# A hybrid attention and delta-rule layer on one core: one chain of delta steps becomes one for each pair of heads, with banks of its own, and input products are computed before their job's phase and places are there

## The chip, the core and the metric

The kernel runs on one NeuronCore of a Trainium2 chip. TensorE multiplies, VectorE and ScalarE do elementwise work and read the accumulator (PSUM, 8 banks of 128 partitions x 512 fp32), GpSimd does elementwise work between tiles in SBUF, and the sync engine (SP) issues nearly all DMAs. The metric is the device time of one execution in microseconds, lower is better. TensorE's clock is throttled at times; the profile gives the granted share.

## What is computed

One layer of a streaming encoder, in fp32, for 2048 prompt frames and 32 sample frames (which have a cache and a state). Both kinds of frames go through one input projection of 6160 columns. Branch A is attention over a band of 576 keys, branch B a gated delta rule in chunks of 64 frames:

```python
qa, ka, va, za, qkv_b, zb, a_b, b_b, gate_a, gate_b = split_projection(x @ w_in)
ya = (band_attention(qa, ka, va) * silu(za)) @ w_branch_a
c = silu(causal_conv(qkv_b)); q, k = l2_normalize(c[q]), l2_normalize(c[k])
m = (k * beta) @ k.T * decay * strict                 # per chunk and head
t_inv = inverse(eye + m); u = t_inv @ (v * beta); w = t_inv @ (k * beta * exp(gc))
def step(s, chunk):                                    # in order over the chunks of a head
    v_new = u - w @ s
    o = (q * exp(gc)) @ s + (q @ k.T * decay) @ v_new
    s = s * exp(g_last) + (k * exp(g_last - gc)).T @ v_new
yb = (rms_norm(o) * silu(zb)) @ w_branch_b
y = layer_norm(ALPHA * x + (sigmoid(gate_a) * ya + sigmoid(gate_b) * yb) @ w_out)
```

## The kernel before

**Halves and phases.** The frames come in two halves of 1024; the 32 sample frames ride with the second. For each half the program opens phase B (`phase_b`, delta rule), runs it to its end, then opens phase A (`phase_a`, attention). After that come the branch projections, the merge and the output projection (`merge`).

**The order is written by a planner when the program is built.** Each activity is a Python generator, a stream with a clock of its own. `Flow.run` always continues the stream whose clock is lowest; an instruction that it issues is appended to its engine's program and moves the stream's clock on by a price. So the planner's clocks set the order of each engine's instructions, and on the chip each engine goes through that order. A stream that yields a `Gate` takes a place (a buffer, a PSUM bank) or waits until one is given back; a `Mark` is an event that it waits for.

**Input products.** `all_jobs` lists jobs of 128 output columns in a fixed order: for each half two or three gate jobs, the job `ab` (decay and beta), the conv jobs of branch B (q, k, v, z for each of the four pairs of heads p) with gate jobs between, six gate jobs, the sixteen jobs of branch A, the rest of the gate jobs. `fetch` loads a job's weights, `divide` splits them into two fp16 parts (`whi`, `wlo`), and `multiply` computes it in blocks of frames: a block is 24 matmuls into a bank `pj` (hi x whi, hi x wlo, lo x whi). There are two such banks. A block's evacuation is a stream of its own that gives the bank back. Counted over the program, the first half's phase B owns blocks 1 to 62, its phase A and the last gate jobs blocks 63 to 100, and the second half's phase B blocks 101 to 195.

A job that belongs to a phase has a key. Before its first block `multiply` itself waits until that phase is open and until the job's places are free (two places `raw_slots` for conv jobs; places for the keys, values, queries and z of branch A).

**Branch B.** `conv` makes q, k, v of a pair (p) and of 512 frames: one of two `Block`s k per pair and half, in all eight per half and one for the sample. `prep` makes decays, `system` the 64x64 systems (block-diagonal tiles `k_bd`, `qk_bd`), `side` the tiles `q_bd`, `kd_bd` and the values `v_t`. `solve` (two streams) inverts the 32x32 halves by substitution on VectorE (`sys_t`, `sys_u`; the data goes over DRAM buffers `sol_p` and `sol_u` to get one row per system), and `inverse` puts the inverse together (`u_bd`) with small matmuls in two banks, one of kind `a` and one of kind `b`. `chain`, one stream for all blocks in `order` (pair after pair), does the steps; `tail` scales and normalises the outputs (square on ScalarE, sums on VectorE, powers and the scaling on GpSimd), transposes them (`ident`, `v_t`) on TensorE, multiplies by z and stores. The last tail ends the phase. Buffers of branch B are chosen by the block's number (`k.n % NSIDE`, `k.n % NPAR`), so they come free in that order.

A step of the chain is, with the name of the tile that each result goes to:

```python
PE.matmul(xs[:, 0:HD], k.kb[:, c, :], st, start=True, stop=True)      # a <- state, k_bd
PE.matmul(os_[:, 0:HD], k.qb[:, c, :], st, start=True, stop=False)    # a <- state, q_bd
V.scalar_tensor_tensor(out=r[:], in0=xs[:, 0:HD], ...)                # r
PE.matmul(ys[:, 0:HD], k.ub[:, c, :], r[:], start=True, stop=True)    # a <- r, u_bd
V.tensor_scalar(out=vn[:], in0=ys[:, 0:HD], ...)                      # vn
PE.matmul(ds_[:, 0:HD], k.kdb[:, c, :], vn[:], start=True, stop=True) # c <- vn, kd_bd
PE.matmul(os_[:, 0:HD], k.qkb[:, c, :], vn[:], start=False, stop=True)# a <- vn, qk_bd
V.scalar_tensor_tensor(out=st, in0=st, ..., in1=ds_[:, 0:HD], ...)    # state
S.copy(out=vc, in_=os_[:, 0:HD])                                      # v_t <- a
```

There are 64 steps in the first half and 68 in the second (four are the sample's). "A hop" below is the way from one of these matmuls over VectorE to the next: over r, over vn, over the state.

**Banks.** The eight banks are set for the whole program: two `pj`, three `a`, two `b`, one `c`. In phase B the chain, the inverse and the tails use `a`, and the systems, the transposes, the weights' scales and the inverse use `b`.

Nearly every instruction is recorded through a helper, so the profile gives line 243 for all of them; the tiles' names tell them apart.

Of the kernel before, what the change touches and what calls it, by code (L numbers as in the profile page):

```python
# [81 lines left out]
class Gate:  # L82
# [169 lines left out]
def trunk(ctx: ExitStack, tc: tile.TileContext, x_p, x_s, cache_k, cache_v, st_conv, st_gdn,  # L252
# [24 lines left out]

    def mark():
        return Mark(flow)
# [5 lines left out]
    banks = {"pj": 2, "a": 3, "b": 2, "c": 1}  # L285
    bank = {k: gate(n) for k, n in banks.items()}

    def pt(tag):

        return psum.tile([P, 512], F32, tag=tag, bufs=banks[tag], name=tag)  # L290
# [252 lines left out]
    class Job:  # L543
# [3 lines left out]
        def __init__(self, half, wid, src, evac=None, key=None, cols=P, blocks=None):  # L547
            self.wid = wid
            self.half, self.src, self.evac, self.cols, self.key, self.slots = half, src, evac, cols, key, ()
# [67 lines left out]

    def multiply():

        while True:  # L620
            some, todo = [], [(0, 0)]
            while todo:
                bi, which = todo.pop(0)
                if which == len(some):
# [36 lines left out]
                flow.start(job.evac(bi, c0, n, gcol, ps))  # L661
# [78 lines left out]
    def phase_b(half):  # L740

        stack = ExitStack()
        bp = stack.enter_context(tc.tile_pool(name=f"bp{half}", bufs=1, reuse_waits="tile"))
# [28 lines left out]
        pd = [dram.tile([32, 1024], F32, name=f"sol_p{half}{i}") for i in range(NSIDE)]  # L772
        ud = [dram.tile([32, 1024], F32, name=f"sol_u{half}{i}") for i in range(NSIDE)]
# [8 lines left out]
        def block(p, b):  # L782
# [4 lines left out]
            k.prep, k.side = mark(), mark()  # L787
# [27 lines left out]
        par_slots, side_slots, u_slots = gate(NPAR), gate(NSIDE), gate(NSIDE)  # L815
        e_slot, tail_slot, p_slots, vt_slots = gate(1), gate(2), gate(NSIDE), gate(NSIDE)
# [177 lines left out]
        def prep():  # L994
            yield decay_done
            for k in order:
# [24 lines left out]
                k.sc = bp.tile([P, 4, 8], F32, tag="sc", bufs=7, name="sc")  # L1021
# [46 lines left out]
        def side(k, ss):  # L1068
# [5 lines left out]
            yield side_slots  # L1074
            k.qb, k.kdb = q_bd[k.n % NSIDE], kd_bd[k.n % NSIDE]
# [27 lines left out]
            yield vt_slots  # L1103
            k.v_t = bp.tile([P, 8, HD], F32, tag="v_t", bufs=NSIDE, name="v_t")
# [17 lines left out]
        def system(k):  # L1122
# [3 lines left out]
            yield par_slots  # L1126
            yield k.qk_ready
            yield k.prep
            yield p_slots
            kb, qkb = k.kb, k.qkb = k_bd[k.n % NPAR], qk_bd[k.n % NPAR]  # L1130
# [1117 lines left out]
```

## Time and profile before

| | us |
|---|---|
| median of 3 runs | 2180.49 |
| lowest, highest | 2174.0, 2183.27 |
| the profiled execution, its own time | 2178.3 |
| its span | 2176.2 |

By the trace, phase B of the first half goes to about 556 us, phase A of the first half to about 862, phase B of the second half to about 1412, and phase A of the second half to about 1800, where the merge has already begun. The rows of the profile are read like this: a group's row has the engine, the operation, tile out <- tiles in, shapes and count, then the busy time, the mean duration of one in ns, and the idle time of the engine just before them with what ended it. A row of the waits is the waiting engine and tile <- what it waited for: the sum, the number of waits, the longest. A row of the windows is a stretch, its length, the busy time and number of instructions for PE, PEld (weight loads), DVE (VectorE), ACT (ScalarE) and POOL (GpSimd), the granted clock of TensorE, the DMA engines' share and GB/s. A row of the timeline is a start, a duration and an instruction, with the wait before it in brackets. An fp32 matmul is recorded as two passes (x2).

### The profile page before, as it was taken

How to read it: one execution, taken by the hardware profiler on the slowest of the kernel's cores; microseconds unless marked ns; L12 is line 12 of the kernel's file. 1: busy time of each engine (PE TensorE's matmuls, PEld its weight loads, DVE VectorE, ACT ScalarE, POOL GpSimd, SP SyncE). 2: the span in 40 equal slices, each digit the busy share in tenths (PEclk: the TensorE clock that was granted, in tenths of full speed). 3: DMA queues.
4: the chain of work that ended last, by engine and by line, in shares of the span. 5: the costliest groups of instructions: out<-in, count | busy, mean ns of one | idle time of the engine just before them, and what ended most of it. 6: DMA issues, size and time to landing. Idle time of an engine off the chain costs nothing. (4 is left out here: it accounts for less than half of the span.)

```text
span 2176.2 us, 41392 instructions
## 1 busy us (share of the span) xinstructions
PE 2008.7 (92%) x15098; PEld 1436.2 (66%) x15098; DVE 1539.9 (71%) x4660; ACT 983.9 (45%) x2098; POOL 634.5 (29%) x708
## 2 busy tenths in 40 slices
PE   4898999999899999898999998899899998999998
PEld 4454665666465556565767776666676777988896
DVE  7689878874377657769887877437557577776676
ACT  5654545444366667554443533345556552111110
POOL 6343333322312123332233331310110214443333
PEclk9999999999999999999999999999999999999999
DMA  3223332332323223122223233231321526443331
GB/s 119 71 83 104 77 86 61 88 88 83 91 77 109 78 88 99 65 69 61 81 58 95 65 91 84 84 107 45 92 68 53 153 76 205 142 129 108 117 104 59
DMA packets 197719, 196.49 MB, mean 90 GB/s; under 512 B 79622, under 2 KB 147570, under 8 KB 197516
## 3 DMA queue, kind: packets, MB, share of 16 engines
q1 hardware_dynamic: 197516, 193.85, 30.4%
q8 instruction: 119, 1.95, 0.4%
q14 instruction: 84, 0.69, 0.1%
HBM read 135.91 MB, written 50.53 MB: 86 GB/s over the span
## 5 line engine op out<-in xcount | busy, mean ns | idle before, releaser
L243 PE MATMUL pj<-hi,whi 128*128 128x512 f16 (+2 forms) x1992 | 659.5, 346 | 16.4 <-ACT raw L243 7.8
L243 PE MATMUL pj<-hi,wlo 128*128 128x512 f16 (+2 forms) x1952 | 649.1, 345 | 0.4 <-POOL wlo L243 0.4
L243 PEld LDWEIGHTS <-whi 128*128 128x128 f16 x3984 | 412.4, 105 | 226.0 <-issue 17.7
L243 PE MATMUL pj<-lo,whi 128*128 128x512 f16 (+2 forms) x1992 | 450.2, 341 | 0.0
L243 POOL TENSOR_TENSOR wlo<-wraw,whi 128x512 f16<-128x512 f32 x192 | 227.9, 1188 | 696.7 <-ACT whi L243 421.5
L243 PEld LDWEIGHTS <-wlo 128*128 128x128 f16 x1952 | 204.7, 105 | 119.9 <-issue 20.9
L243 ACT CAST mh<-sg 128x256 fp32r<-128x256 f32 x64 | 25.9, 406 | 276.0 <-DVE sg L243 276.0
L243 DVE TENSOR_TENSOR sys_u<-sys_u,sys_t 128x60 f32<-128x60 f32 (+24 forms) x527 | 134.2, 255 | 18.5 <-DVE sys_t L243 0.2
L243 ACT ACTIVATE wraw<-wraw,w_scale 128x1024 f32<-128x1024 f32 (+1 forms) x98 | 111.5, 1137 | 63.1 <-DVE w_scale L243 62.6
L243 PE MATMUL a<-ghi,whi 128*128 128x256 f32 (+1 forms) x512 | 132.3, 289 | 7.6 <-DVE sg L243 7.4
L243 ACT CAST whi<-wraw 128x512 f16<-128x512 f32 (+1 forms) x196 | 119.3, 611 | 30.6 <-PE pj L243 28.0
L243 ACT CAST ph<-b 128x512 f16<-128x512 f32 (+2 forms) x224 | 92.9, 422 | 86.8 <-PE b L243 78.9
L243 PE MATMUL a<-ghi,wlo 128*128 128x256 f32 (+1 forms) x512 | 130.2, 285 | 0.6 <-DVE wlo L243 0.5
L243 DVE TENSOR_TENSOR pl<-b,ph 128x512 f16<-128x512 f32 (+2 forms) x224 | 106.8, 484 | 26.3 <-ACT ph L243 25.6
L243 DVE TENSOR_TENSOR sys_t<-sys_u,sys_p 128x60 f32<-128x60 f32 (+21 forms) x459 | 118.4, 258 | 4.7
L243 ACT ACTIVATE sb<-sb,mx,unit 128x640 f32<-128x640 f32 (+4 forms) x128 | 108.8, 851 | 27.7 <-DVE mx L243 25.8
L243 DVE SCALAR_TENSOR_TENSOR acc<-raw,cwT,acc 128x512 f32<-128x512 f32 x144 | 113.2, 786 | 6.0 <-ACT acc L243 5.0
L243 ACT COPY v_t<-a 128x64 f32<-128x64 f32 x132 | 27.9, 211 | 192.6 <-PE a L243 184.0
L243 POOL TENSOR_TENSOR w_scale<-w_scale,mhalf 128x1 f32<-128x1 f32 x49 | 30.3, 618 | 287.3 <-DVE w_scale L243 219.2
L243 PE MATMUL b<-ident,sb 128*128 128x128 f32 x560 | 100.0, 279 | 14.1 <-ACT sb L243 6.2
L243 PEld LDWEIGHTS a<-ghi,whi 128*128 128x128 f32 x512 | 97.7, 191 | 9.6 <-DVE sg L243 8.5
L243 PEld LDWEIGHTS a<-ghi,wlo 128*128 128x128 f32 x512 | 97.3, 190 | 1.3 <-DVE wlo L243 1.0
(356 smaller groups left out, 4270.5 us busy)
## 6 DMA issues: line engine op xcount, KB each, us to landing
wraw<-in_w_in SPq DMA_DIRECT2D x192, 256.0 KB
sg<-sig SPq DMA_DIRECT2D x112, 128.0 KB
sig<-sig SPq DMA_DIRECT2D x44, 256.0 KB
sys_p<-sol_p SPq DMA_DIRECT2D x17, 512.0 KB
x<-in_x_p SPq DMA_DIRECT2D x16, 512.0 KB
xt<-in_x_p SPq DMA_DIRECT2D x16, 512.0 KB
out_y_p<-xt SPq DMA_DIRECT2D x16, 512.0 KB
glo<-g SPq DMA_DIRECT2D x14, 512.0 KB
```

What stands on the lines that cost most here:

```text
L243: r = f(*a, **k)
```

## The change

**Banks by phase.** Only `pj` and `b` (two each) stay for the whole program. The other four are opened with a stage: three `a` at the start and three `a` and one `c` in phase A as before, and in phase B two `x` and two `o`.

**A chain for each pair of heads.** The single stream becomes four (one for each pair's two blocks) and one for the sample. A chain takes one of two numbered places before a block and with it one bank `x`, in which the step's three results have columns of their own, and one bank `o` for the output. The two matmuls on the output, and ScalarE's copy, are no longer issued by the chain but by short streams beside it (`outputs`). Since blocks can now end in another order, buffers are handed out as numbered places and given back by number, the buffers in DRAM are one for each block, and three small tiles have more buffers.

**Products before phase and places.** `multiply` no longer waits for a job's phase and places. It starts a stream that does (`open_job`), and the block's evacuation waits for that, with its bank.

**The inverse** uses one bank `b` for both heads in place of an `a` and a `b`, and the tails use `b`.

```diff
+class Places(Gate):
+    def __init__(self, flow, n):
+        super().__init__(flow, n)
+        self.numbers = deque(range(n))
+    def take(self):
+        yield self
+        return self.numbers.popleft()
+    def back(self, i):
+        self.numbers.append(i)
+        self.give()
...
-    banks = {"pj": 2, "a": 3, "b": 2, "c": 1}
+    banks = {"pj": 2, "b": 2}
...
+    def open_job(job):
+        go, make = phases[job.key[0]][job.half]
+        yield go
+        job.evac, slots = make[0](*job.key[1:])
+        for g in slots:
+            yield g
+        job.open.done()
+
+    def evac(job, *block):
+        if job.key:
+            yield job.open
+        yield from job.evac(*block)
...
                     if job.key:
-                        go, make = phases[job.key[0]][job.half]
-                        yield go
-                        job.evac, job.slots = make[0](*job.key[1:])
-                    for g in job.slots:
-                        yield g
+                        job.open = mark()
+                        flow.start(open_job(job))
...
-                flow.start(job.evac(bi, c0, n, gcol, ps))
+                flow.start(evac(job, bi, c0, n, gcol, ps))
...
+        open_banks(stack, f"psb{half}", x=2, o=2)
...
-        pd = [dram.tile([32, 1024], F32, name=f"sol_p{half}{i}") for i in range(NSIDE)]
+        pd = [dram.tile([32, 1024], F32, name=f"sol_p{half}{i}") for i in range(2 * NP)]
...
-            yield side_slots
-            k.qb, k.kdb = q_bd[k.n % NSIDE], kd_bd[k.n % NSIDE]
+            k.sn = yield from side_slots.take()
+            k.qb, k.kdb = q_bd[k.sn], kd_bd[k.sn]
...
-            banks_ = []
+            yield bank["b"]
+            ps = pt("b")
             for h in range(2):
                 r0 = h * HD
-                yield bank["ba"[h]]
-                ps = pt("ba"[h])
-                banks_.append(ps)
...
+        def outputs(m, x, os_, vc=None, end=None):
+            PE.matmul(os_, m, x, start=vc is None, stop=vc is not None)
+            yield
+            if vc is not None:
+                S.copy(out=vc, in_=os_)
+                if end:
+                    end.done()
+
-        def chain():
-            for k in order:
+        def chain(some):
+            for k in some:
                 yield k.ready
+                xn = yield from x_banks.take()
...
+                xs, ys, ds_ = (xb[xn][:, i * HD:(i + 1) * HD] for i in range(3))
+                os_ = ob_[xn][:, 0:HD]
                 for c in range(k.nch):
...
+                    PE.matmul(xs, k.kb[:, c, :], st, start=True, stop=True)
+                    yield
+                    r = bp.tile([P, HD], F32, tag=f"r{xn}", bufs=2, name="r")
+                    V.scalar_tensor_tensor(out=r[:], in0=xs, scalar=k.negc[:, c:c + 1], in1=vc, op0=ALU.mult, op1=ALU.add)
+                    yield
+                    PE.matmul(ys, k.ub[:, c, :], r[:], start=True, stop=True)
+                    flow.start(outputs(k.qb[:, c, :], st, os_))
+                    yield
+                    vn = bp.tile([P, HD], F32, tag=f"vn{xn}", bufs=2, name="vn")
+                    V.tensor_scalar(out=vn[:], in0=ys, scalar1=sc[:, 1, c:c + 1], scalar2=None, op0=ALU.mult)
+                    yield
+                    PE.matmul(ds_, k.kdb[:, c, :], vn[:], start=True, stop=True)
+                    flow.start(outputs(k.qkb[:, c, :], vn[:], os_, vc, k.out if c == k.nch - 1 else None))
+                    V.scalar_tensor_tensor(out=st, in0=st, scalar=sc[:, 3, c:c + 1], in1=ds_, op0=ALU.mult, op1=ALU.add)
+                    yield
+                yield k.out
+                x_banks.back(xn)
...
-        for g in (worker(todo), worker(decays), prep(), local(), solve(), solve(), chain()):
+        for g in (worker(todo), worker(decays), prep(), local(), solve(), solve()):
             flow.start(g)
+        for some in blocks + ([[sample]] if last else []):
+            flow.start(chain(some))
```

What this does to the order of TensorE is seen at two places. The first is the end of the first half's phase B. Before, these are the last matmuls of the chain (its last step and a part of the one before) and the last tail's transposes, with the first product of branch A behind them:

```order
L243 MATMUL b<-w_sq,tiny 128x1
L243 MATMUL c<-vn,kd_bd_618 128x64
L243 MATMUL a<-vn,qk_bd_608 128x64
L243 MATMUL a<-state,k_bd_600 128x64
L243 MATMUL a<-state,q_bd_612 128x64
L243 MATMUL a<-r,u_bd_624 128x64
L243 MATMUL c<-vn,kd_bd_618 128x64
L243 MATMUL a<-vn,qk_bd_608 128x64
L243 MATMUL a<-ident,v_t 128x128 x4
L243 LDWEIGHTS whi
L243 MATMUL pj<-hi_147,whi 128x512
```

Now the last step of the chain stands among products:

```order
L259 MATMUL o<-state,q_bd_619 128x64
L259 LDWEIGHTS whi
L259 MATMUL pj<-hi_150,whi 128x512
L259 MATMUL x<-vn,kd_bd_625 128x64
L259 LDWEIGHTS wlo
L259 MATMUL pj<-hi_150,wlo 128x512
L259 MATMUL o<-vn,qk_bd_615 128x64
L259 LDWEIGHTS whi
L259 MATMUL pj<-hi_150,whi 128x512
```

and the transposes of the last tail follow 35 products later:

```order
L259 LDWEIGHTS whi
L259 MATMUL pj<-lo_153,whi 128x512
L259 MATMUL b<-ident,v_t_655 128x128 x4
L259 LDWEIGHTS whi
L259 MATMUL pj<-lo_153,whi 128x512
```

What moved: the steps' two last matmuls, on `kd_bd` and `qk_bd`, are apart, and products stand between the chain's end and the transposes. At that place 62 blocks of products had been begun before and 60 are now; at the last transposes of the second half 195 before and 191 now.

The second place is a change from one block to the next in the middle of the first half, with the buffers' numbers. Before, the last step of a block (`c_4421`, `a_4396`) ends before the next block's first matmul (`a_4435`):

```order
L243 MATMUL c_4421<-vn_4415,kd_bd0_616 128x64
L243 MATMUL a_4396<-vn_4415,qk_bd3_608 128x64
L243 LDWEIGHTS whi_4017
L243 MATMUL pj_4403<-hi01_149,whi_4017 128x512
L243 LDWEIGHTS wlo_4018
L243 MATMUL pj_4403<-hi01_149,wlo_4018 128x512
L243 LDWEIGHTS whi_4017
L243 MATMUL pj_4403<-hi01_149,whi_4017 128x512
L243 LDWEIGHTS wlo_4018
L243 MATMUL pj_4403<-hi01_149,wlo_4018 128x512
L243 MATMUL a_4435<-state_118,k_bd0_594 128x64
```

Now the next block's first step (in bank `x_659`) stands beside the last step of the block before (in bank `x_660`):

```order
L259 MATMUL x_660<-state_118,k_bd3_607 128x64
L259 LDWEIGHTS whi_3829
L259 MATMUL pj_4084<-lo00_151,whi_3829 128x512
L259 MATMUL x_659<-state_118,k_bd0_601 128x64
L259 LDWEIGHTS whi_3829
L259 MATMUL pj_4084<-lo00_151,whi_3829 128x512
L259 MATMUL x_660<-r_4189,u_bd0_629 128x64
L259 LDWEIGHTS whi_3829
L259 MATMUL pj_4084<-lo00_151,whi_3829 128x512
L259 MATMUL o_662<-state_118,q_bd0_617 128x64
L259 MATMUL x_659<-r_4197,u_bd1_631 128x64
```

What moved: two blocks have a step beside each other here. Over the whole of the first half the first matmuls of the steps come as eight of one block, then eight of the next, as before.

More of the change, by code (lines that the diff above doesn't have):

```diff
@@ L1102, in side @@
             yield from by_token(k.qk[:, 1, :], nch, put_k)
-            yield vt_slots
-            k.v_t = bp.tile([P, 8, HD], F32, tag="v_t", bufs=NSIDE, name="v_t")
+            k.vn = yield from vt_slots.take()
+            k.v_t = v_ts[k.vn]
             yield bank["b"]
@@ L1205, in inverse @@
         def inverse(k, t):
-            yield u_slots
-            k.ub = u_bd[k.n % NSIDE]
+            k.un = yield from u_slots.take()
+            k.ub = u_bd[k.un]
             nch, ub, p_c = k.nch, k.ub, k.p_c
-            u0 = ud[k.n % NSIDE][:]
+            u0 = ud[k.n % (2 * NP)][:]
             yield t
@@ L1361, in tail @@
                 yield t
-            vt_slots.give()
+            vt_slots.back(k.vn)
             if k.p is None:
@@ L1367, in tail @@
             tail_slot.give()
-            if k is order[-1]:
+            left[0] -= 1
+            if not left[0]:
                 done.done()
```

101 lines of the change are left out of this document (45 added, 56 removed).

## The prediction

> **What bounds the kernel now.** I read the page first, then the table of windows cut at the borders of the stages, then the waits and the timeline at the places that these point to.
>
> ```profile
> span 2176.2 us, 41392 instructions
> PE 2008.7 (92%) x15098; PEld 1436.2 (66%) x15098; DVE 1539.9 (71%) x4660; ACT 983.9 (45%) x2098; POOL 634.5 (29%) x708
> ```
>
> TensorE is busy for 2008.7 of 2176.2 us. So all that this change can win is in the other 167.5 us, in time at a lower clock, and in matmuls that take longer than they must. It acts in the two stages of branch B, from about 100 to 562 us and from about 900 to 1414 us:
>
> ```profile
> 200.00:440.00 240.00, 220.64 (x1591) 145.65 (x1590) 203.48 (x715) 115.26 (x236) 76.22 (x103) 0.96 0.32 82
> 440.00:545.00 105.00, 101.22 (x784) 69.38 (x783) 60.89 (x250) 42.74 (x92) 30.26 (x31) 0.98 0.29 85
> 545.00:562.00 17.00, 9.34 (x38) 5.32 (x39) 5.39 (x19) 4.42 (x9) 9.33 (x9) 0.70 0.34 96
> ...
> 1010.00:1150.00 140.00, 129.53 (x1056) 95.78 (x1054) 125.63 (x428) 65.29 (x144) 42.72 (x63) 0.93 0.27 74
> 1150.00:1350.00 200.00, 187.64 (x1586) 143.67 (x1585) 156.56 (x565) 81.09 (x186) 58.70 (x75) 0.96 0.31 82
> ...
> 1400.00:1414.00 14.00, 7.87 (x45) 4.52 (x44) 6.60 (x21) 3.08 (x6) 7.71 (x8) 0.76 0.25 69
> ```
>
> The columns after the length are the busy time of PE, PEld, DVE, ACT and POOL, then the granted clock. Each stage has three parts. In the first, VectorE is nearly as full as TensorE: 203.48 of 240 us beside 220.64, and 125.63 of 140 beside 129.53. In the second, VectorE has room (60.89 of 105 us in the first half's stage) and TensorE alone sets the pace. In the third, 545 to 562 and 1400 to 1414, neither is full: the input products are used up and TensorE waits for the last block's tail. So a term that takes work from TensorE pays fully in the second part only, and work of VectorE that moves from the second part into the first costs up to its whole length.
>
> **The change, term 1: the waits at the end of both stages go.**
>
> ```profile
> 544.70:555.60 10.90, 3.09 (x19) 2.38 (x18) 4.69 (x18) 4.72 (x9) 5.53 (x5) 0.76 0.27 84
> 555.60:561.40 5.80, 5.73 (x18) 2.67 (x19) 0.88 (x2) 0.00 (x0) 3.80 (x5) 0.57 0.41 94
> 561.40:565.00 3.60, 3.60 (x18) 1.65 (x17) 0.00 (x0) 0.69 (x1) 0.00 (x0) 1.00 0.13 51
> ...
> 1402.20:1408.30 6.10, 0.04 (x1) 0.00 (x0) 2.66 (x8) 2.46 (x5) 3.88 (x4) 0.90 0.27 66
> 1408.30:1413.10 4.80, 4.73 (x24) 2.61 (x25) 2.85 (x10) 0.00 (x0) 3.82 (x5) 0.50 0.32 109
> ```
>
> ```profile
> 555.67 1.11 PE L243 MATMUL a<-ident,v_t 128*128 128x128 f32 x4 [6.60 <-POOL v_t L243]
> 1408.37 1.60 PE L243 MATMUL a<-ident,v_t 64*64 64x64 f32 x16 [6.13 <-POOL v_t L243]
> ```
>
> Both rows are transposes of a tail, which wait for the tail's scaling on GpSimd. In the old order of TensorE nothing stands between the last delta step of the first half and these transposes, and all 62 blocks of products of that stage are already behind it; in the second half it is 195 of 195. The next product belongs to branch A, and it waited for the phase. In the new order 35 product matmuls stand between the last step and the last transposes of the first half, and 36 and 45 before those of the sample rows. A product takes 0.2 us at the full clock (3.60 us for 18), so 35 are 7.0 us, against the 6.60 us of the wait; the last two steps, which stood bare, have products between them too. In the second half most products are narrower, so 36 and 45 of them may leave 1 or 2 us of the 6.13. What is gained: idle 10.90 − 3.09 = 7.8 us and 6.10 − 0.04 = 6.1 us, and the work after them at a lower clock, 5.73 × (1 − 0.57) = 2.5 us and 4.73 × (1 − 0.50) = 2.4 us. Together **−18.7 us**. What is late next there is nothing: branch A's first scores wait for products 70 and 207 in both orders, which TensorE now reaches sooner by as much.
>
> On the lower clock the rows have 5.8 and 4.8 us at about half speed behind each wait. The Trainium skill, "TensorE: Matmul & The Clock Gate", section "Part 1: The HAM clock gate", says that the full clock returns after one busy window of about 3.4 us. By that an estimate of each wait's aftermath would be 1.7 us and the term −17.3 us; the trace's longer stretch decides here.
>
> **Term 2: two matmuls of a step no longer stand side by side.**
>
> ```profile
> 302.85 0.36 PE L243 MATMUL c<-vn,kd_bd 128*128 128x64 f32 x2
> 303.05 0.39 PE L243 MATMUL a<-vn,qk_bd 128*128 128x64 f32 x2
> 303.27 0.38 PE L243 MATMUL pj<-hi,wlo 128*128 128x512 f16 x1
> ...
> 304.14 0.33 PE L243 MATMUL a<-state,k_bd 128*128 128x64 f32 x2
> 304.31 0.38 PE L243 MATMUL pj<-hi,wlo 128*128 128x512 f16 x1
> ```
>
> ```profile
> L243 PE MATMUL c<-vn,kd_bd 128*128 128x64 f32 x264 | 52.7, 282 | 16.1 <-DVE vn L243 11.3 <-DVE w_scale L243 4.4
> L243 PE MATMUL a<-vn,qk_bd 128*128 128x64 f32 x264 | 52.5, 282 | 0.0
> L243 PE MATMUL a<-r,u_bd 128*128 128x64 f32 x264 | 48.9, 268 | 23.0 <-DVE r L243 17.8 <-DVE sys_t L243 3.7 <-ACT zb L243 0.8
> L243 PE MATMUL a<-state,k_bd 128*128 128x64 f32 x256 | 44.7, 257 | 1.5 <-DVE state L243 1.2
> L243 PE MATMUL a<-state,q_bd 128*128 128x64 f32 x256 | 44.4, 256 | 0.1
> ```
>
> A step's matmul on kd_bd and the one on qk_bd followed each other and hold TensorE from 302.85 to 303.27, 0.42 us. One of the same shape between two products holds it for 0.17 us (304.14 to 304.31), so two apart take 0.34. The new order has them apart in all 132 steps, nearly always with a product between. That is 132 × 0.08 = 10.6 us by these rows; by the groups it is (52.7 + 52.5) − (44.7 + 44.4) × 264/256 = 13.3 us. I take 13 as the whole, and count half, **−6.5 us**, because in the first part of each stage TensorE's own time isn't what ends last. The other half is the bound below.
>
> **Term 3: VectorE's work comes earlier.** I counted the chain's steps and the finished systems in both orders at the same block of products. At block 54 of the first half there were 42 steps and now are 49, and one system more is finished (each system is one run of sys_t and sys_u); at block 188 it is 129 steps for 120, and half a system more.
>
> ```profile
> L243 DVE TENSOR_SCALAR vn<-a,sc 128x64 f32<-128x64 f32 x132 | 37.0, 280 | 31.3 <-PE a L243 29.8
> L243 DVE SCALAR_TENSOR_TENSOR r<-a,negc,v_t 128x64 f32<-128x64 f32 x132 | 37.0, 280 | 31.4 <-PE a L243 29.6
> L243 DVE TENSOR_TENSOR sys_u<-sys_u,sys_t 128x60 f32<-128x60 f32 (+24 forms) x527 | 134.2, 255 | 18.5 <-DVE sys_t L243 0.2
> L243 DVE TENSOR_TENSOR sys_t<-sys_u,sys_p 128x60 f32<-128x60 f32 (+21 forms) x459 | 118.4, 258 | 4.7
> ```
>
> A step has three operations like the first two rows (the third updates the state), 3 × 0.28 = 0.84 us; a system takes (134.2 + 118.4) / 17 = 14.9 us. So 7 × 0.84 + 14.9 = 20.8 us of VectorE's work come forward in the first half and 9 × 0.84 + 7.5 = 15.0 us in the second, 35.8 us in all, out of the part where they lay beside products into the part where VectorE is nearly full. What hides them there is VectorE's idle time, 36.5 us (240 − 203.48) and 43.4 us (200 − 156.56). That this is real room is seen in what it waits for:
>
> ```profile
> DVE state L243 <- PE c L243: 19.5, 32, 1.9
> DVE r L243 <- PE a L243: 18.4, 23, 1.6
> DVE vn L243 <- PE a L243: 13.1, 19, 1.6
> DVE sys_t L243 <- DMA sys_p<-sol_p: 10.0, 3, 4.1
> ```
>
> These are VectorE's waits from 100 to 556 us. 51.0 us of them are for TensorE, in 74 short pieces, and a VectorE that is later finds TensorE's result there. The bounds are 0 and +35.8 us. Since the room is twice the work, I take a quarter, **+9 us**.
>
> **Term 4: hops of the chain with less beside them.**
>
> ```profile
> 544.22 0.33 PE L243 MATMUL a<-state,k_bd 128*128 128x64 f32 x2
> 544.59 0.28 DVE L243 SCALAR_TENSOR_TENSOR r<-a,negc,v_t 128x64 f32<-128x64 f32 x1 [0.97 <-PE a L243]
> 545.02 0.41 PE L243 MATMUL a<-r,u_bd 128*128 128x64 f32 x2 [0.24 <-DVE r L243]
> ```
>
> Here, with VectorE free, the hop from one matmul of a step over VectorE to the next takes 0.80 us, and 0.24 of it is a wait. In the old order 44 of the 395 hops have under 0.5 us of TensorE's work between their matmuls, in the new one 66 have. With two products there (0.17 + 2 × 0.2 = 0.57 us) up to 0.23 us is missing: 22 × 0.23 = 5 us. A hop can also turn out better, where VectorE's queue puts the operation sooner. Bounds −4 and +8; I take **+3 us**.
>
> **What I cost at nothing.**
>
> ```profile
> PE pj L243 <- ACT raw L243: 4.4, 1, 4.4
> L243 ACT ACTIVATE wraw<-wraw,w_scale 128x1024 f32<-128x1024 f32 (+1 forms) x98 | 111.5, 1137 | 63.1 <-DVE w_scale L243 62.6
> ```
>
> An evacuation that waits for its place now holds one of the two product banks, and the product after next is queued behind it on TensorE. But that wait is there before as well (first row, 960 to 1415 us: a product waits 4.4 us for the evacuation into raw), because the same tile has to be free; only what stands beside it in the order differs. A chain now keeps one accumulator: its matmul on q_bd waits for ScalarE's copy of the step before, and behind it stand one product and the chain's next matmul. The copy has the rest of a step, some 2 us, and ScalarE is 45% busy; behind its longest operation (1.14 us, second row) it still comes in time. Without that cover it would cost up to 1.1 us a step. One bank for two in the inverse, places by number and 16 solver buffers for 3 move no work. "Side by side" too I cost at nothing: in the new order the steps still come in whole runs of eight, block after block, and two blocks touch only in the last step of one and the first of the next. When a block is ready, not the chain, sets its start.
>
> **The sum.** −18.7 − 6.5 + 9 + 3 = −13.2 us. The profiled execution took 2178.3 us (span 2176.2), so 2165.1; the median of the three runs shown is 2.2 us above it, so **2167 us**, 0.6% under the median of 2180.5. A measurement of this kernel can tell about 0.5%, 11 us, from no change.
>
> **Rivals.**
>
> VectorE takes the early work in whole, and TensorE's saving pays everywhere: term 3 is 0, term 2 is −13, term 4 is 0. −31.7 us, **2149 us**. For it: the 51 us of waits for TensorE. Against: 125.63 of 140 us from 1010 to 1150.
>
> What the ends give is taken back in the middle: term 3 costs half of its upper bound, 18 us, and term 2 is worth nothing. −18.7 + 18 = about 0, **2180 us**. It is also the case in which the change doesn't do what it says, since no chain gets shorter and one idle time is only exchanged for another. For it: both orders have the same work, and the chains don't overlap.
>
> VectorE becomes the bound in the first part of both stages: its whole 35.8 us stay visible, TensorE waits for r and vn, term 2 is worth nothing: −18.7 + 35.8 + 3 = +20 us, **2200 us**, slower. It decides from the point where VectorE's idle time in 200 to 440 us can't fall under the 36 us of now, that is if its waits are of the queue's order rather than for results. For it: TensorE already waits for VectorE in these parts, for r and vn for 29.1 us (17.8 + 11.3) in all. Against: the 51 us that VectorE itself waits for TensorE from 100 to 556 us.
>
> **Chances.** The forecast 0.40, all hidden 0.25, no net change 0.22, slower 0.13. The forecast's own range is 2158 to 2176 by half of term 3's and term 4's bounds; some 0.24 of its 0.40 is faster by over 0.5% (under 2169.6). So faster 0.49 (0.25 + 0.24), within 0.5% 0.36, slower by over 0.5% 0.15. The range reaches from the lowest sum (−18.7 − 13 − 4, or 2145) to the slower case at 2200.
>
> **What would show it.** Term 1: the transposes of v_t at the ends have no wait over 1 us and the clock doesn't fall there. Term 2: the group on qk_bd has a mean near 257 ns. Term 3: from 200 to 440 us VectorE's share rises over 85% and its waits for TensorE fall under 51 us; if instead TensorE's waits for r, vn and sys_t rise well over 29 us, the slower rival holds. Term 4: many waits of 0.1 to 0.3 us before u_bd. Wrong altogether it would be if branch A or the merge, where I changed nothing, took another time.

## The result

| | us | ratio to before | 95% interval |
|---|---|---|---|
| before, median of 4 runs | 2177.24 | | |
| after, median of 4 runs | 2118.36 | 0.9729 | 0.9695 to 0.9762 |
| after, once more, median of 5 runs (before: 2179.17) | 2123.45 | 0.9735 | 0.9707 to 0.9763 |

The change gains 56 to 59 us, more than four times the 13 that were forecast. These are the first lines of the page of after:

```profile
span 2123.1 us, 41363 instructions
PE 1994.4 (94%) x15098; PEld 1422.5 (67%) x15098; DVE 1534.2 (72%) x4660; ACT 978.7 (46%) x2098; POOL 634.3 (30%) x708
```

The same 15098 matmuls are 14.3 us shorter in sum (2008.7 before), and TensorE is without work for 128.7 us in place of 167.5. Work and idle time together make the 53.1 us between the two spans.

To see where they went, I cut both executions where TensorE begins the same input product (number 1488, 2600, 3200, 4720 and 5925 of the 5936 product matmuls that each trace has; these stand near the borders of the stages). The windows of before:

```profile
0.00:561.80 561.80, 492.65 (x3315) 312.83 (x3316) 425.30 (x1390) 275.85 (x532) 200.80 (x249) 0.95 0.30 86
561.80:895.10 333.30, 320.68 (x2436) 195.05 (x2435) 222.44 (x769) 205.13 (x429) 75.37 (x80) 0.99 0.29 88
895.10:1012.40 117.30, 104.00 (x762) 69.48 (x761) 85.25 (x203) 65.99 (x117) 34.83 (x60) 0.96 0.22 66
1012.40:1424.10 411.70, 382.23 (x3178) 286.76 (x3176) 312.35 (x1103) 171.29 (x386) 122.05 (x157) 0.95 0.29 80
1424.10:1747.90 323.80, 305.79 (x2752) 215.25 (x2751) 196.46 (x669) 184.86 (x431) 45.22 (x40) 0.99 0.29 84
1747.90:2176.20 428.30, 403.35 (x2663) 356.87 (x2663) 298.12 (x529) 80.76 (x205) 156.18 (x123) 0.98 0.38 119
```

And of after, cut at the same products:

```profile
0.00:548.70 548.70, 489.45 (x3316) 309.27 (x3317) 426.79 (x1390) 272.63 (x530) 198.90 (x247) 0.97 0.30 87
548.70:873.50 324.80, 317.96 (x2435) 193.94 (x2434) 221.49 (x769) 206.05 (x432) 76.18 (x82) 0.99 0.31 93
873.50:978.00 104.50, 100.97 (x761) 68.22 (x760) 76.41 (x178) 63.29 (x113) 36.68 (x60) 0.98 0.24 69
978.00:1390.40 412.40, 381.25 (x3183) 278.07 (x3182) 318.57 (x1130) 173.04 (x391) 121.71 (x157) 0.98 0.30 80
1390.40:1701.50 311.10, 306.15 (x2822) 218.90 (x2821) 200.35 (x693) 188.32 (x443) 45.03 (x40) 1.00 0.32 90
1701.50:2123.10 421.60, 398.66 (x2590) 354.07 (x2588) 290.56 (x504) 75.31 (x192) 155.84 (x123) 0.98 0.38 119
```

By stage, after minus before: branch B of the first half (from the start) −13.1, branch A of the first half −8.5, the first 600 product matmuls of branch B in the second half −12.8, its rest +0.7, branch A of the second half −12.7, everything behind −6.7. The prediction looked at the middles and the ends of branch B. Over half of the gain, 27.9 us, lies in branch A and behind it, where it expected nothing, and 12.8 us at a start that it didn't cost. The same stretches for the kernels of the experiments, each minus before, in us:

| kernel | B, 1st half | A, 1st half | B, 2nd half, start | its rest | A, 2nd half | behind |
|---|---|---|---|---|---|---|
| after | −13.1 | −8.5 | −12.8 | +0.7 | −12.7 | −6.7 |
| products_only | −25.4 | +7.2 | −14.5 | −5.9 | −9.4 | −4.9 |
| chains_only | −12.9 | −0.1 | −0.6 | +6.3 | +6.6 | −2.4 |
| a_waits | −13.6 | +1.2 | −11.1 | −1.5 | −0.5 | −1.3 |
| b_waits | −12.0 | −3.2 | +2.0 | +4.3 | −10.2 | −7.9 |
| late_evac | −16.2 | +6.3 | +3.5 | −13.3 | +18.2 | −20.9 |
| before_raw3 | −8.0 | −0.1 | −14.4 | +4.1 | −1.1 | −3.3 |
| v_waits | −17.7 | −8.5 | −12.8 | −2.4 | −1.0 | +1.4 |

Each row is one execution. Where the last products of a kernel stand late among branch A's matmuls, as in late_evac, the last two columns are to be read together.

### The wait that I had cost at nothing

The start of the second half shows it best. The waits of TensorE in that stretch of before (895.1 to 1012.4 us) begin with this row (the waiting engine and tile, what it waited for, us in total, times, the longest):

```profile
PE pj L243 <- ACT raw L243: 7.8, 2, 4.4
```

and after has none for `raw` there. The timeline of ScalarE in before shows why, and of TensorE the instruction that waits:

```profile
941.02 0.72 ACT L243 ACTIVATE acc<-raw,cwT 128x512 f32<-128x512 f32 x1 [0.32 <-DVE qk_s L243]
944.13 0.63 ACT L243 ACTIVATE e<-acc 128x512 f32<-128x512 f32 x1 [2.39 <-DVE acc L243]
946.00 0.72 ACT L243 ACTIVATE acc<-raw,cwT 128x512 f32<-128x512 f32 x1 [1.24 <-DVE qk L243]
946.63 0.67 ACT L243 ACTIVATE raw<-pj,w_inv 128x512 f32<-128x512 f32 x1
...
947.35 0.38 PE L243 MATMUL pj<-hi,whi 128*128 128x272 f16 x1 [3.44 <-ACT raw L243]
```

The same place in after:

```profile
921.12 0.72 ACT L259 ACTIVATE acc<-raw,cwT 128x512 f32<-128x512 f32 x1 [0.32 <-DVE qk_s L259]
921.75 0.67 ACT L259 ACTIVATE raw<-pj,w_inv 128x512 f32<-128x512 f32 x1
924.23 0.63 ACT L259 ACTIVATE e<-acc 128x512 f32<-128x512 f32 x1 [1.82 <-DVE acc L259]
924.77 0.47 ACT L259 ACTIVATE raw<-pj,w_inv 128x272 f32<-128x272 f32 x1
```

The first row is the same operation in both. In after the evacuation into `raw` (`raw<-pj`) stands right behind it and waits for nothing, so the place is free by then. In before it stands two operations further back, behind two that wait for VectorE (2.39 and 1.24 us), and TensorE waits 3.44 us for the bank that it empties. The planner let `multiply` begin the product only when the place came free, so it dated the evacuation one whole product block later, and put ahead of it on ScalarE's queue what by its dates was ready sooner. After the change the product is dated as done when the place comes free, and the evacuation is put there.

### The profile page after: what moved, and what is told of

The parts are those of the page before. It is cut to its first block, busy times and chain, and to the rows that moved or that the text cites. A ratio compares the mean times of both kernels' runs of the same rounds, so it can differ in the third digit from the quotient of the medians.

```text
span 2123.1 us, 41363 instructions
## 1 busy us (share of the span) xinstructions
PE 1994.4 (94%) x15098; PEld 1422.5 (67%) x15098; DVE 1534.2 (72%) x4660; ACT 978.7 (46%) x2098; POOL 634.3 (30%) x708
## 5 line engine op out<-in xcount | busy, mean ns | idle before, releaser
L259 PE MATMUL pj<-hi,whi 128*128 128x512 f16 (+2 forms) x1992 | 650.7, 342 | 8.6 <-POOL whi L259 3.0
L259 PE MATMUL pj<-hi,wlo 128*128 128x512 f16 (+2 forms) x1952 | 640.8, 341 | 0.4 <-POOL wlo L259 0.4
L259 PE MATMUL pj<-lo,whi 128*128 128x512 f16 (+2 forms) x1992 | 461.9, 340 | 0.0
L259 DVE TENSOR_TENSOR sys_u<-sys_u,sys_t 128x60 f32<-128x60 f32 (+24 forms) x527 | 135.7, 258 | 18.2
L259 DVE TENSOR_TENSOR sys_t<-sys_u,sys_p 128x54 f32<-128x54 f32 (+21 forms) x459 | 123.6, 269 | 4.0
L259 ACT COPY v_t<-o 128x64 f32<-128x64 f32 x132 | 27.5, 209 | 158.3 <-PE o L259 121.5
```

The source lines that it names most:

```text
L259: r = f(*a, **k)
```

## The experiments

All ratios are to runs of the kernel before on the same chip.

| kernel | us | ratio, 95% interval |
|---|---|---|
| products_only | 2125.10 | 0.9765, 0.9738 to 0.9792 |
| chains_only | 2174.71 | 0.9982, 0.9965 to 0.9999 |
| a_waits | 2150.69 | 0.9876, 0.9853 to 0.9899 |
| b_waits | 2152.84 | 0.9889, 0.9863 to 0.9915 |
| go_waits | 2126.56 | 0.9750, 0.9721 to 0.9778 |
| late_evac | 2156.56 | 0.9888, 0.9858 to 0.9917 |
| before_raw3 | 2154.77 | 0.9886, 0.9855 to 0.9917 |
| products_raw3 | 2124.59 | 0.9755, 0.9728 to 0.9782 |
| v_early | 2172.89 | 0.9978, 0.9956 to 1.0001 |
| v_waits | 2137.14 | 0.9824, 0.9797 to 0.9851 |
| before_kqv | 2168.46 | 0.9964, 0.9947 to 0.9982 |
| one_chain | 2115.41 | 0.9704, 0.9674 to 0.9733 |
| adjacent | 2122.95 | 0.9750, 0.9724 to 0.9776 |
| pj3 | 2120.26 | 0.9733, 0.9709 to 0.9757 |
| one_chain_kqv | 2126.76 | 0.9781, 0.9755 to 0.9807 |

### Which half of the change

`products_only` is the kernel before with the new `open_job` and `evac` and the few lines of `multiply`. `chains_only` is after with the wait put back:

```diff
                         flow.start(open_job(job))
+                        yield job.open
```

> The kernel before with the change to the products alone: multiply no longer waits for phase and places, the evacuation does; the chain is one stream with the old banks. Theory (the planner's waits dated every block of a job with a key, and so its evacuation's place in ScalarE's order, by the free place and not by the product's end; all the gain lies there): the four pieces read from the two traces, 18.7 at the ends of branch B, 11.6 at the start of its second half, 21.9 in branch A, 8.5 behind the last product, less some overlap: 2120 to 2140 us. Rival (the four chains with their own banks bring it): 2165 to 2180.

> The changed kernel, but multiply waits for the job's phase and places as before; four chains, x and o banks, numbered places, one bank for the inverse stay. Theory (all of the gain lies with the products): 2165 to 2185 us, within some 10 us of before. Rival (the chains bring it): 2115 to 2135.

2125.1 and 2174.7 us: both as the theory said. The products bring 53 us and the chains 3 or 4.

### Which jobs

The same line, under `if job.key[0] == 0:` for branch A's jobs and `== 1` for branch B's. `go_waits` puts back the wait for the phase alone.

```diff
                         flow.start(open_job(job))
+                        yield phases[job.key[0]][job.half][0]
```

> The changed kernel, but multiply waits for phase and places where the job belongs to branch A (16 jobs in each half). Theory: the ends of branch B come back (the first job of A waits for its phase; 18.7 us with the low clock behind them), and so does what the trace shows in branch A and behind the last product (6.5 + 15.4 + 8.5): 2145 to 2170 us. Rival (branch A is faster only because branch B ends earlier or in another order): only the ends come back, 2130 to 2140. Rival (the chains): 2115 to 2122.

> The changed kernel, but multiply waits for phase and places where the job belongs to branch B. Theory: the 11.6 us at the start of the second half come back, in the first half next to nothing, so 2125 to 2135 us, and in the trace TensorE waits for raw's evacuation again at the start of the second half's branch B (7.8 us before). Rival (that start is faster for the chains' sake): 2115 to 2122.

> The changed kernel, but multiply waits for the job's phase, not for its places. The prediction put 18.7 us on the end of the phase; with the waits of branch A's jobs restored the trace showed no TensorE wait there (1.3 and 0 us of idle time). Theory (places count, the phase doesn't): 2115 to 2128 us. Rival (the phase): 2135 to 2150.

Branch A's waits cost 27 to 32 us (2150.7 against the two medians of after) and branch B's 29 to 34, at least twice what I expected of branch B's. a_waits lies in its range, but not by its sum: the 18.7 us at the ends of branch B stayed away, and against after the table has 9.7 and 12.2 us more in the two branches A and 5.4 behind. The two together come to more than all the waits at once, which cost 51 to 56 us in chains_only, so they overlap. For b_waits the stages show 14.8 us at the start of the second half, near what I expected, and 2 to 5 us in its rest and in each branch A that I didn't. The phase alone is worth nothing that these intervals can tell, 2126.6 us.

### The place in ScalarE's order, or in TensorE's

`late_evac` lets the products start without their places and dates the evacuations as late as before:

```diff
             yield job.open
+            yield job.open.at + 5.1 * (block[0] + 1)
         yield from job.evac(*block)
```

> The changed kernel, products dated as early as there, but the planner dates the evacuation of a job with a key not before 5.1 us (one product block by its prices) per block behind the free place, where the kernel before had it. Nothing on the chip waits for longer because of it; only the evacuation's place in ScalarE's order, and what follows from it, is later. Theory (that place is what the change gained by): most of the 56 us go, 2150 to 2175 us. Rival (the gain is TensorE's own order: products early as fill between branch B's and A's small matmuls): 2115 to 2130.

2156.6 us, 33 to 38 us of the gain are gone. By the stages they are gone in branch A of the first half, 6.3 us longer than in before, at the start of the second half, 3.5 longer, and from branch A there to the end, 2.7 shorter where after is 19.4 shorter. TensorE's waits at that start (885.2 to 1006 us) are led by the old row again:

```profile
PE pj L259 <- ACT raw L259: 8.3, 3, 3.7
```

So some 60% of the gain hangs on the evacuations' dates. But the edit moves TensorE's order too: a block keeps its bank until its evacuation, so in the plan the products behind it come late as well. Ahead of product 3600 TensorE has done 3836 other matmuls in late_evac, 3740 in after and 3826 in before. How much of the 60% is the place in ScalarE's order, and how much TensorE's own order behind it, this run doesn't tell. The other 24 us stay, by the stages in branch B of the first half and in its rest in the second.

### The same cure without the change

`before_raw3` gives the kernel before a third place `raw`; `products_raw3` does so with the early products.

```diff
-        raw_slots, qk_slots, v_slots = gate(2), gate(NQK), gate(2)
+        raw_slots, qk_slots, v_slots = gate(3), gate(NQK), gate(2)
...
-                raw = bp.tile([P, 3 + HALF], F32, tag="raw", bufs=2, name=f"raw{p}{i}")
+                raw = bp.tile([P, 3 + HALF], F32, tag="raw", bufs=3, name=f"raw{p}{i}")
...
-                    raw_s = bp.tile([P, 3 + DEC], F32, tag="raw_s", bufs=2, name=f"raws{p}{i}")
+                    raw_s = bp.tile([P, 3 + DEC], F32, tag="raw_s", bufs=3, name=f"raws{p}{i}")
```

> The kernel before with three places raw in place of two and nothing else: the planner's wait of branch B's conv jobs for a place becomes rarer without any edit to multiply. Theory (the planned wait for raw costs 10 to 20 us in branch B): 2155 to 2170 us, the gain at the start of the second half. Rival (the wait for raw is free, the products gain for another reason): 2174 to 2182.

> The kernel before with the change to the products and a third place raw: two cures of one wait. Theory (the wait for the place is the cause of both gains, 53 and 26 us alone): they don't add up, 2105 to 2126 us. Rival (two causes): their sum, 2095 to 2103.

2154.8 us, at the lower edge of the theory's range: one more buffer and no edit to the products gives 1.14%, some 25 us, 14.4 of them at the start of the second half, where the change gave 12.8, and the wait for `raw` is gone from TensorE's list there. With both, 2124.6 us: they don't add up, so what the third place cures is among what the early products cure.

### Branch A

In the planner's run of before, `multiply` waits for a place of branch A only five times: twice for z in the first half, and three times in the second half for the one place of the values (`vf_slot`, jobs v of pairs 1 to 3). `v_early` frees only these jobs from the wait, `v_waits` puts only these waits back into after (`job.key[0] == 0 and job.key[1] > 0 and job.key[2] == 0`), and `before_kqv` turns the order of the jobs so that k and q no longer stand behind them.

```diff
-                for i, f in enumerate((8, 4, 0, 12)):
+                for i, f in ((1, 4), (2, 0), (0, 8), (3, 12)):
```

> The kernel before, in which only the products of the values' jobs of pairs 1 to 3 in branch A no longer wait for their place. Theory (branch A's gain comes from this one place): its second half 10 to 16 us shorter, branch B as before, 2155 to 2170 us. Rival (branch A gains by other places too, or by what branch B leaves to it): 2172 to 2182.

> The changed kernel, in which only the products of the values' jobs of pairs 1 to 3 in branch A wait for their place. Theory (as above): as with all of branch A's jobs waiting, 2140 to 2152 us. Rival: 2113 to 2128.

> The kernel before with branch A's jobs of a pair in the order k, q, v, z in place of v, k, q, z: the wait for the values' place no longer holds the products of k and q. Theory (what the wait costs is what stands behind it in the one stream of products): 2155 to 2172 us. Rival (only the values' own evacuation counts): 2174 to 2184.

v_waits is 2137.1 us, under the range expected and above the rival's: the one place makes about half of what branch A's jobs give (14 to 19 of 27 to 32 us). The rest I didn't split; it is the z places and the phase, or what comes with them. In the waits of TensorE in branch A of the second half, before (1424.1 to 1747.9 us) and v_waits (1382.7 to 1705.5 us) have the same row at the head,

```profile
PE b L243 <- ACT sb L243: 6.2, 3, 2.1
PE b L243 <- DVE pl L243: 5.1, 6, 1.4
```

```profile
PE b L259 <- ACT sb L259: 6.2, 3, 2.1
PE b L259 <- DVE pl L259: 5.9, 6, 1.6
```

three waits of about 2 us for an exponential on ScalarE, as many as there are late v jobs. After has 0.2 us of it in that stage, and no row there over 1.3.

By its time alone v_early missed: 2172.9 us, not told from before. Its windows say more, up to the end of branch B, branch A of the second half, and behind:

```profile
0.00:1430.50 1430.50, 1306.64 (x9685) 868.56 (x9686) 1044.89 (x3464) 718.25 (x1464) 433.57 (x546) 0.95 0.29 83
1430.50:1754.30 323.80, 312.17 (x2851) 222.56 (x2850) 202.24 (x700) 189.78 (x446) 45.43 (x40) 0.99 0.30 87
1754.30:2172.90 418.60, 395.37 (x2566) 352.56 (x2563) 287.38 (x498) 74.33 (x190) 155.36 (x123) 0.97 0.37 120
```

Up to 1430.5 its TensorE has the very order of before, and yet it is there 6.4 us later (before is there at 1424.1), at a lower clock, 0.95 for 0.96. From there on, where the edit is, it is 9.7 us shorter (742.4 us against 752.1), all of it in the last window. That agrees with the theory, but it isn't shown by the time. before_kqv at 2168.5 us is as expected, a small gain.

### What the chains and banks are worth

`one_chain` starts `chain(order)` once. `adjacent` issues the matmul on `qk_bd` right behind the one on `kd_bd`, and only the copy stays in `outputs`. `pj3` has three banks `pj`, one `x`, two `o` and in branch A two `a`. `one_chain_kqv` is one_chain with the turned order of jobs.

```diff
-        for some in blocks + ([[sample]] if last else []):
-            flow.start(chain(some))
+        flow.start(chain(order))
...
-                    flow.start(outputs(k.qkb[:, c, :], vn[:], os_, vc, k.out if c == k.nch - 1 else None))
+                    PE.matmul(os_, k.qkb[:, c, :], vn[:], start=False, stop=True)
+                    flow.start(outputs(os_, vc, k.out if c == k.nch - 1 else None))
...
-    banks = {"pj": 2, "b": 2}
+    banks = {"pj": 3, "b": 2}
```

The first piece is one_chain's, the second adjacent's, the third pj3's.

> The changed kernel with a single chain over all blocks in the old order (its two places x and o stay, so a block may begin in the other bank). Theory (the chains hardly run side by side, they are worth nothing): 2113 to 2128 us. Rival (two chains fill each other's hops): 2130 to 2150.

> The changed kernel with the matmul on qk_bd issued right behind the one on kd_bd in all 132 steps, as before the change (now they are adjacent in 2). Theory of the prediction's second term (TensorE holds the pair about 0.1 us longer when the two are adjacent, 13 us whole, half of it on the path): 2124 to 2133 us. Rival (TensorE has the room, or the pair's cost only moves): 2113 to 2123.

> The changed kernel with three banks pj, paid for with one bank x (the chains take turns, the step's output alternates between two banks o) and with one bank a less in branch A. Theory (products that are held with their bank until their evacuation can start want banks): 2095 to 2115 us if the two chains and the third bank a are worth as little as the one chain was, over 2130 if branch A wants its third a.

> The kernel with one chain and early products, with branch A's jobs in the order k, q, v, z. Theory (a v product that waits with its bank for the place still holds one of the two banks pj, so k and q ahead of it help a little): 2105 to 2116 us. Rival (nothing is left there): 2113 to 2122.

One chain does as well as five: 2115.4 us is the fastest time here, though its interval (0.9674 to 0.9733) touches that of after (0.9707 to 0.9763), so I don't call it faster. adjacent is after within the interval. A third bank `pj` in place of an `x` and an `a` wins nothing: pj3's 2120.3 us are after's, and neither of its two forecasts held. one_chain_kqv is 11 us slower than one_chain and outside both of its forecasts; once the products don't wait, the values do better first. Why, no run here tells.

## Why the prediction was wrong

**The step that failed** is the one on the evacuations: "But that wait is there before as well (…), because the same tile has to be free; only what stands beside it in the order differs." On the chip that is true, and it costs nothing. But the wait in `multiply` was the planner's, not the chip's, and what it moved was the order of ScalarE behind it. I had the row, 4.4 us for `raw`, and took it for the price of a full tile. (Its window began at 960 us, so it left out the 3.44 us at 947.) It was the price of a queue: the place was free while ScalarE waited for VectorE ahead of the evacuation. Here is the evacuation of that row in before,

```profile
1007.10 0.63 ACT L243 ACTIVATE e<-acc 128x512 f32<-128x512 f32 x1 [4.39 <-DVE acc L243]
1007.63 0.67 ACT L243 ACTIVATE raw<-pj,w_inv 128x512 f32<-128x512 f32 x1
```

and in after it stands ahead of that wait. The table of stages shows the size. What I had costed (the parts of branch B behind its first 600 product matmuls in each half) came to about −6 us for the −13.2 of the sum, and what I had put at nothing, with the clock that goes with it, to −47. That the cause is the planner's waits in `multiply` is shown by the runs above; that all of the −47 goes by ScalarE's order isn't, since TensorE's order moves with it. The prediction named the sign by which this is known, "if branch A or the merge, where I changed nothing, took another time". The change's lines do act there: all of branch A's jobs have keys.

**Term 1** (−18.7): the waits went, and the clock is full there. These are the middle and the end of each stage of branch B, cut at the same products (600, 1400 and 1488; 3600, 4400 and 4720). Before:

```profile
198.80:519.60 320.80, 297.89 (x2221) 198.29 (x2220) 255.92 (x928) 150.10 (x310) 101.75 (x129) 0.96 0.31 82
519.60:561.80 42.20, 34.31 (x197) 22.55 (x196) 15.03 (x57) 12.66 (x26) 14.84 (x14) 0.88 0.32 95
1130.80:1345.00 214.20, 200.00 (x1667) 151.55 (x1665) 170.36 (x608) 89.25 (x201) 66.16 (x83) 0.96 0.33 87
1345.00:1424.10 79.10, 72.45 (x598) 53.27 (x596) 36.27 (x139) 27.88 (x64) 20.63 (x19) 0.96 0.29 83
```

After:

```profile
192.10:528.50 336.40, 313.34 (x2352) 212.00 (x2351) 273.41 (x986) 153.22 (x324) 104.10 (x130) 0.96 0.29 80
528.50:548.70 20.20, 20.20 (x98) 9.35 (x97) 3.70 (x14) 8.24 (x13) 11.46 (x12) 1.00 0.43 132
1095.80:1325.70 229.90, 213.73 (x1866) 158.91 (x1864) 194.24 (x709) 95.22 (x220) 68.12 (x85) 0.98 0.30 82
1325.70:1390.40 64.70, 64.70 (x489) 45.61 (x489) 17.47 (x63) 22.96 (x50) 17.91 (x18) 1.00 0.33 96
```

TensorE's idle time at the two ends was 7.9 and 6.7 us and is 0, so 14.5 us for the 13.9 that were forecast. The reason given isn't needed, though. The waits are all but gone in chains_only and in a_waits too, where branch A's products still wait for their phase. Here is the end of the first half's stage in chains_only, with 1.3 us of idle time:

```profile
525.60:549.10 23.50, 22.21 (x121) 12.07 (x120) 6.64 (x28) 9.64 (x17) 6.28 (x7) 1.00 0.35 114
```

The other half of the change does it alone: when the first half's product 1400 begins, TensorE has 1782 of its other matmuls behind it in chains_only, 1720 in before.

**Term 3** (+9): VectorE did take the work, as this window of after shows (215.34 of 240 us, 90%, where over 85% was foretold):

```profile
200.00:440.00 240.00, 220.47 (x1665) 149.15 (x1663) 215.34 (x758) 114.34 (x240) 80.59 (x108) 0.95 0.28 79
```

Its price was near what was forecast. The two middles are 15.6 and 15.7 us longer than before, but nearly all of that is TensorE's own work, which moved there from the ends: 131 and 199 more matmuls, 15.5 and 13.7 us more busy time. TensorE's idle time there rose by 0.2 and 2.0 us, and by 6.4 in the stretch ahead of the second (products 3200 to 3600, from 8.6 to 15.0), 8.5 us together, with term 4 in it. So the rival "what the ends give is taken back in the middle" holds for the second half alone (6.7 us of idle time gone at the end, 8.4 come back); chains_only, 3 us under its before, is near that rival's time.

**Term 2** (−6.5, whole −13) is nothing. The groups of after,

```profile
L259 PE MATMUL x<-r,u_bd 128*128 128x64 f32 x264 | 54.2, 288 | 19.1 <-DVE r L259 11.9 <-DVE sys_t L259 5.1 <-ACT whi L259 0.9
L259 PE MATMUL x<-vn,kd_bd 128*128 128x64 f32 x264 | 51.9, 279 | 15.8 <-DVE vn L259 15.4
L259 PE MATMUL x<-state,k_bd 128*128 128x64 f32 x256 | 50.2, 279 | 8.6 <-DVE state L259 8.1
L259 PE MATMUL o<-vn,qk_bd 128*128 128x64 f32 x264 | 44.6, 251 | 0.0
L259 PE MATMUL o<-state,q_bd 128*128 128x64 f32 x256 | 44.0, 254 | 0.9 <-ACT v_t L259 0.8
```

show the mean for qk_bd at 251 ns, as foretold, 282 before. But k_bd went from 257 to 279 and u_bd from 268 to 288, and the five groups sum to 244.9 us against 243.2. The saving in one pair was paid in others, and adjacent, which undoes it, costs nothing. Nor did the fuller clock at the ends show in the sum: over the costed parts TensorE's busy time is 0.3 us longer than before, where these two had −11.4 (the first half's part now holds 32 small matmuls that stood ahead of it). That makes the −6 us: −14.5 at the ends, +8.5 in the middles, +0.3.

**Term 4** (+3) lay within its bounds, but not where it was named: TensorE's waits for r, vn, state and sys_t are 11.9 + 15.4 + 8.1 + 5.1 = 40.5 us, against 17.8 + 11.3 + 1.2 + 3.7 = 34.0 before, 6.5 more, and those before u_bd (for r) fell while those for the state rose. The rivals of 2149 and 2200 us fell; VectorE didn't become the bound.

**The clock** I counted only at the two ends (4.9 us). By the mean granted clock, 0.971 of 2176.2 us and 0.980 of 2123.1, before loses 63.1 us to the lower clock and after 42.5. A part of that falls on idle time, where it costs nothing; counted only where TensorE works, the traces have 55.2 and 37.5 us. So some 18 of the 53 us are this by the clock, and 14.3 by the busy time of the same matmuls, spread over the stages.

## What to carry to other kernels

In a program whose order is written by a planner, look for waits that exist only in the planner: a stream that waits for a buffer before it issues the work ahead of the buffer's writer dates that writer too late, and the writer can then stand in its engine's queue behind work that isn't ready. Let the producer run ahead with its own accumulator and put the wait on the one instruction that needs the buffer; a third buffer at the place that is waited for gave nearly half as much here with an edit of three numbers. When an edit applies to all jobs of a kind, cost it at every stage where such jobs stand, not only where the change's name points.

## What the runs showed of the hardware

A longer wait of TensorE is often paid for twice. The end of a 2.68 us wait for `r` at 1098.51 us of before and what follows it, in windows:

```profile
1098.51 0.43 PE L243 MATMUL a<-r,u_bd 128*128 128x64 f32 x2 [2.68 <-DVE r L243]
```

```profile
1098.50:1099.40 0.90, 0.89 (x5) 0.57 (x6) 0.86 (x3) 0.00 (x0) 0.00 (x0) 1.00 0.21 33
1099.40:1104.00 4.60, 4.60 (x19) 2.87 (x18) 4.22 (x17) 0.42 (x2) 0.00 (x0) 0.63 0.58 157
1104.00:1108.00 4.00, 4.00 (x34) 3.11 (x32) 2.45 (x12) 2.02 (x4) 0.00 (x0) 1.00 0.38 74
```

TensorE works without a gap for 4.60 us at a clock of 0.63, 1.7 us lost. From 100 us on, all seven waits of before that last 3 us or more have such a stretch, begun in the wait or just behind it. Of the shorter ones some are and some aren't: after the 2.43 us for r that end at 216.6 us, and after each of the three of some 2.1 us in branch A of the second half, the clock stays at 1.00. The trace's record of the clock has nothing between half and full speed, and before's 27 stretches at half speed last 3.41 us (17 of them), 6.83 (9) or 10.24 (1). So the loss comes in steps of 1.7 us, and isn't the same each time. One wait for vn stands at the same place of the same order in before, here with the window behind it,

```profile
467.79 0.43 PE L243 MATMUL c<-vn,kd_bd 128*128 128x64 f32 x2 [3.30 <-DVE vn L243]
```

```profile
468.00:472.00 4.00, 4.00 (x18) 2.74 (x18) 1.78 (x9) 0.21 (x1) 0.00 (x0) 0.57 0.64 171
```

and in v_early, likewise:

```profile
471.27 0.69 PE L243 MATMUL c<-vn,kd_bd 128*128 128x64 f32 x2 [4.02 <-DVE vn L243]
```

```profile
470.00:478.00 8.00, 6.73 (x26) 4.69 (x27) 3.72 (x19) 0.43 (x2) 0.00 (x0) 0.57 0.36 99
```

4.00 × 0.43 = 1.7 us in the one. In the other TensorE works for 6.73 of the 8.00 us, so some 6.73 × 0.43 = 2.9 us; its wait was also 0.7 us longer. The Trainium skill, "TensorE: Matmul & The Clock Gate", section "Part 1: The HAM clock gate", says that activity is judged in windows of about 3.4 us that run freely and don't start with the kernel. The steps agree with half the clock for one or two such windows (half of 3.4 is 1.7).

Much of the scatter between runs goes with this. In 23 runs of before on one chip the span went from 2165.7 to 2184.1 us and the clock from 0.974 to 0.964, but span times clock only from 2105.5 to 2114.8. That product scatters half as much as the time: before 2110, chains_only 2118, v_early 2096, before_raw3 2101, after 2081, one_chain 2084 (medians). It leaves out what a change does to the clock, so it doesn't rank the kernels by time: chains_only is not slower than before. Why v_early's clock is lower (median 0.965 against 0.970) while it waits less, no run tells.
